# Decoder block on one core: pooling and gate arithmetic of VectorE dealt out in pieces, and nine low weight parts taken from the DMA to VectorE

## The chip, the core and the metric

The kernel runs on one core of a Trainium2 chip. A core has TensorE (PE) for matrix products, VectorE (DVE), ScalarE (ACT) and GpSimd (POOL) for element-wise work, SyncE (SP) which here only starts transfers, and 16 DMA engines. Each engine takes its instructions strictly in the order in which the program lists them, and waits on semaphores for what other engines or transfers have to finish first. The metric is the device time of one execution in microseconds, lower is better.

## What is computed

One block of a hybrid decoder on 528 positions (16 learned meta tokens and 512 real ones) of width 1024. Cut to what matters for the change, with its names:

```python
p = rmsnorm(h) @ w_in
q, k, v, glr, r, u, ga, gb = split(p)
o = gated_linear_attention(q, k, v, glr)            # chunks of 64, four heads
y_a = (rmsnorm(o) * silu(r)) @ w_a
# four groups of 256 channels, trailing mean over 2, 4, 8, 16 positions, minus the token
pooled = [mean_w(u[g]) - u[g] for g, w in enumerate((2, 4, 8, 16))]
y_b = (concat(pooled[g] @ w_pool_grp[g]) * pool_scale) @ w_b
h = h + (sigmoid(ga + b_a) * y_a + sigmoid(gb + b_b) * y_b) @ w_o
up = causal_conv3(rmsnorm(h) @ w_up)
h = h + (silu(up[:, :2816]) * up[:, 2816:]) @ w_down
out = rmsnorm(h)[16:]
```

All of it is float32. To get this accuracy from TensorE, an operand is split into a high part, which is its rounding to `fp32r`, and a low part, which is the operand minus the high part; a product is then three products: high by high, high weight by low data, low weight by high data.

## The kernel before, in words

Channels lie on the 128 partitions and positions on the free axis. The program has three stretches: projections for the attention (k, q, v, r) and the attention itself, then a list of units called `seq`, and at the end the last parts of the down product and the final norm. The change is in the units.

**Units.** A unit makes 256 output channels. Its number below is its place in `seq`: 0 is u0, 1 to 3 are a0 to a2, 4 is u1, 5 is u2, 6 is a3, 7 is u3, 8 to 11 are ga0 to ga3, 12 to 14 are gb0 to gb2, 15 is the grouped product grp, 16 is b0, 17 is gb3, 18 to 20 are b1 to b3, 21 to 24 are o0 to o3, and from 25 on come the 22 up units with the down units among them. A number after a name in the rows below (`gl10`, `sh_10a`, `x9`) is the number of the unit it belongs to; the profile itself leaves most of these numbers out.

**Plain and fast units.** A `plain` unit (L663) does eight products over two column halves. A `fast` unit (L695) is one level of a Strassen-like scheme: seven block products in place of eight, made by `seven`, into four PSUM banks `x`, `y`, `q` and `v`. Banks `x` and `q` are used more than once: the product into `x` that begins the unit (weights `gh` and `gl`) is read out by ScalarE (L710, "z11"), and only when it has been read does the second product into `x` (weights `sh_…a` and `sl_…a`) go on from the bank's contents. The same holds for L713 (z22), L716 (z12), L718 and L720 on VectorE, and L722 (z21) at the unit's end.

**Weights of a unit.** `fetch` loads a unit's raw weights (1 MB) into one of three buffers `raw`. `make_high` rounds three of its four blocks into `gh` on ScalarE (L607). `make_low` makes the low part `gl`: ScalarE writes the negated high part into it (L597), and three transfers started by GpSimd add the raw weights onto it from DRAM (L599, `accum_op=add`). `make_sums` makes the block sums: four additions in place on VectorE (L624), then high parts `sh_…a`, `sh_…b` on ScalarE and low parts `sl_…a`, `sl_…b` on VectorE (L269 and L270, the two lines of the helper `split`). `gh`, `gl` and the `s` tiles have two buffers each, so `sh_…b` of a unit cannot be written before the unit ahead of it is done with its own.

**When they are made.** In unit n, `fast` asks for the high part and the sums of unit n+1 behind z11, and `prepare` asks for the low part of unit n+2 behind z21. Between these edges the scheduler of the framework sets the order on each engine from the order of the code and its own estimate of times.

**Pooling and gates.** `pool_tree(g)` runs on VectorE behind a u unit: g+1 additions of shifted copies (L768), for g = 3 also two short operations (L766, L771), then the mean minus the token (L773), and `split` into `pah` on ScalarE and `pal` on VectorE. In the ga units VectorE also multiplies `ya` by the gate (L862), behind the sigmoids of ScalarE (L787).

**The start.** VectorE and GpSimd add up the squares for the first norm (L246 to L248); GpSimd also fills four constant tiles there (L299 to L301 and L309).

Of the kernel before, what the change touches and what calls it, by code (L numbers as in the profile page):

```python
# [1 line left out]

# [9 lines left out]
I32 = mybir.dt.int32  # L12
AF = mybir.ActivationFunctionType
ALU = mybir.AluOpType
# [4 lines left out]
T0 = 14  # L19
# [20 lines left out]
CROSS_X = {(0, 0): 0, (0, 1): 1, (1, 0): 2, (1, 1): 3}  # L40
# [30 lines left out]
def f32(ap):  # L71
    return ap.bitcast(F32)
# [3 lines left out]
def hybrid_block(ctx: ExitStack, tc: tile.TileContext, xt, g1d, wts, wsq, wdown, wglr, wgk, vecs, out):  # L76
    nc = tc.nc
    act, dve, pool, pe, sp = nc.scalar, nc.vector, nc.gpsimd, nc.tensor, nc.sync
# [153 lines left out]
    sq1 = big("sq1")  # L232
# [12 lines left out]
    for k in (2, 4, 6):  # L245
        pool.tensor_tensor(sq1[0], sq1[0], sq1[k], ALU.add)  # L246
        dve.tensor_tensor(sq1[1], sq1[1], sq1[k + 1], ALU.add)
    dve.tensor_tensor(sq1[0], sq1[0], sq1[1], ALU.add)  # L248

    def rsqrt_mean(dst, acc, cols, n, tmp):  # L250
        for src, c in parts_of(acc, cols):
# [16 lines left out]
    def split(hi, lo, src):  # L268
        act.activation(hi, src, AF.Copy)  # L269
        dve.tensor_tensor(lo, src, f32(hi), ALU.subtract)  # L270
# [25 lines left out]
    e1, e2 = flat("early1", lastp), flat("early2", lastp)  # L296
    reset, gk, kend0 = e1[:, 0:L], e1[:, 528:1040], e2[:, 0:512].rearrange("p (h c) -> p h c", h=4)
    glr_raw = e2[:, 512:640].rearrange("p (k c) -> p k c", k=KT)
    pool.memset(reset, 1.0)  # L299
    pool.memset(reset[:, 16 : 16 + 3 * 128 + 1 : 128], 0.0)  # L300
    pool.memset(gk, 0.0)  # L301
    for i in range(6):
        sp.dma_start(gk[16 * i : 16 * i + 16], wgk)
    sp.dma_start(vec, vecs)
# [1 line left out]
    glr_w = flat("glr_w", lastp, F32R, 1024).rearrange("p (k c) -> p k c", k=KT)  # L306
    gkg = flat("gkg", lastp, F32R)
    gk_r, glr = gkg[:, 0:512], gkg[:, 512:1040]
    pool.memset(glr_w.bitcast(I32), 0)  # L309
    stack = glr_w[:, :, 0:96].rearrange("p k (j i c) -> p k j i c", j=3, i=2)  # L310
    raw3 = glr_raw.unsqueeze(2).to_broadcast([P, KT, 3, 16])
    act.activation(stack[:, :, :, 0], raw3, AF.Copy)
# [5 lines left out]
    for k in range(KT):  # L318
        for m in range(2):
            hi, lo = preps[m]  # L320
# [95 lines left out]
    o = Whole("o")  # L416
# [129 lines left out]
    seq = [("plain", "u", 0)] + [("plain", "a", i) for i in range(3)]  # L546
# [11 lines left out]
    loaded, own, sums = {}, {}, {}  # L558
# [17 lines left out]
    low_made, high_made = set(), set()  # L576

    def direct_tiles(n):
# [9 lines left out]
                own[n] = [blocks(t) for t in hl], hl, None  # L588
        return own[n]

    def make_low(n):
        if n >= len(seq) or seq[n][0] == "down" or n in low_made:
            return
        low_made.add(n)
        _, (hi, lo), _ = direct_tiles(n)
        kind, name, i = seq[n]
        act.activation(lo, loaded[n][:, 0:3], AF.Copy, scale=-1.0)  # L597
        for b in (2, 0, 1) if kind == "fast" else (0, 1, 2) if name == "grp" else (1, 2, 0):
            pool.dma_start(lo[:, b], wsq[UNIT[name] + i, :, b], accum_op=ALU.add)  # L599

    def make_high(n):
        if n >= len(seq) or n in high_made:
            return
        high_made.add(n)
        _, (hi, lo), k = direct_tiles(n)
        if k is None:
            act.activation(hi, loaded[n][:, 0:3], AF.Copy)  # L607
        else:
            split(hi, lo, loaded[n].rearrange("p a b -> p (a b)")[:, 0:k])

# [3 lines left out]
    def make_sums(n):  # L614
        if n >= len(seq) or n in sums or seq[n][0] == "down":
            return
        raw = loaded[n]
        if seq[n][0] == "plain":
            x = two(f"{n}x")
            split(*(t[:, 0:1] for t in x), blocks(raw[:, 3:4]))  # L620
            sums[n] = (x,)
            return
        for dst, x in ((0, 3), (3, 2), (2, 0), (1, 2)):
            dve.tensor_tensor(raw[:, dst], raw[:, dst], raw[:, x], ALU.add)  # L624
        sums[n] = (two(f"{n}a"), two(f"{n}b"))
        split(*sums[n][0], blocks(raw[:, 0:3:2]))
        split(*sums[n][1], blocks(raw[:, 1:4:2]))
# [13 lines left out]
    def prepare(n, ins=None):  # L641
        fetch(n + 2)
        fetch(n + 3)
        behind(ins, make_low, n + 2)
# [24 lines left out]
    def plain(n, i, xh, xl, cols, evict, cross=None):  # L669
        w = weights(n)  # L670
        make_high(n + 1)
        make_sums(n + 1)
        for c in range(2):
            evict(2 * i + c, plain_half(n, i, c, xh, xl, cols, w))
            if cross and (i, c) in cross[0]:
                cross[1](cross[0][i, c])
        prepare(n)

    def lattice(name, b, n, x):
# [12 lines left out]
    def seven(acc, w, block, x, at, n, first=True):  # L692
        for k in range(4):
            for e, (a, b) in enumerate(((0, 0), (0, 1), (1, 0))):
                pe.matmul(  # L695
                    acc[:, 0:n], w[a][:, block, k], x[k][b][:, at],
                    start=first and k == 0 and e == 0, stop=k == 3 and e == 2,
                    skip_group_check=not first,
                )

    def fast(n, z, sides, cols):
        direct, crossed = sides
        g, sa, sb = weights(n)
        z11, z12 = (z[:, 0, a:b] for a, b in cols)
        z21, z22 = (z[:, 1, a:b] for a, b in cols)
        x, y, q, v_ = (bank(f"{c}{n}") for c in "xyqv")
        w = cols[0][1] - cols[0][0]
        n_ = slice(0, w)
        seven(x, g, 2, direct, 2, w)
        behind(act.activation(z11, x[:, n_], AF.Copy), make_high, n + 1)  # L710
        make_sums(n + 1)
        seven(q, sa, 0, crossed, 1, w)
        act.activation(z22, q[:, n_], AF.Copy)  # L713
        seven(v_, g, 0, crossed, 3, w)
        seven(x, sa, 1, crossed, 2, w, False)
        act.activation(z12, x[:, n_], AF.Copy)  # L716
        seven(y, g, 1, direct, 0, w)
        dve.tensor_tensor(z11, y[:, n_], z11, ALU.add)  # L718
        seven(q, sb, 0, direct, 1, w, False)
        dve.tensor_tensor(z12, q[:, n_], z12, ALU.add)  # L720
        seven(x, sb, 1, crossed, 0, w, False)
        turned = act.activation(z21, x[:, n_], AF.Copy, scale=-1.0)  # L722
        dve.tensor_tensor(z22, z21, z22, ALU.subtract)
        dve.tensor_tensor(z21, v_[:, n_], z21, ALU.add)
        prepare(n, turned)
# [5 lines left out]
    pah, pal = big("pah", F32R, lastp), big("pal", F32R, unitp)  # L731
# [18 lines left out]
        sides_x[1].append(x)  # L750

    def pool_tree(g):
        cur = u.pair(g)
        need = T0
        starts = []
        for i in reversed(range(g + 1)):
            starts.append(need)
            need = max(0, need - (1 << i))
        starts = starts[::-1]
        temps = big(f"pt{g}", F32, lastp if g < 3 else unitp)  # L760
        for i in range(g + 1):
            d = 1 << i
            nxt = temps.pair(i % 2)
            a = starts[i]
            if a < d:
                dve.tensor_copy(nxt[:, :, a:d], cur[:, :, a:d])  # L766
                a = d
            dve.tensor_tensor(nxt[:, :, a:], cur[:, :, a:], cur[:, :, a - d : L - d], ALU.add)  # L768
            cur = nxt
        if g == 3:  # L770
            dve.tensor_scalar(cur[:, :, T0 : T0 + 1], cur[:, :, T0 : T0 + 1], 16.0 / (T0 + 1), None, ALU.mult)  # L771
        ug = u.pair(g)[:, :, T0:]
        dve.scalar_tensor_tensor(ug, cur[:, :, T0:], 1.0 / (2 << g), ug, ALU.mult, ALU.subtract)  # L773
        split(pah.pair(g)[:, :, T0:], pal.pair(g)[:, :, T0:], ug)

    def take_u(m, accs):
        scaled(u[m], accs, HALF)
# [62 lines left out]
    for n in range(len(seq)):  # L840
        kind, name, i = seq[n]
        if name == "up":
            break
        if name == "u" and kind == "plain":
            for k in range(4):
                load_x(k)
            plain(n, i, xh, xl, HALF, take_u)
            ya = Whole("ya")
        elif name == "a":
            plain(n, i, zh, zl, TAIL, take_a, (CROSS_X, cross_x))  # L850
            if i == 2:
                pool_tree(0)
            if i == 3:
                pool_tree(2)
        elif name == "u":
            fast(n, u.pair(i), sides_x, FULL)
            if i != 2:
                pool_tree(i)
        elif name == "ga":
            z, _ = unit_gate(n, i, name)  # L860
            y = ya.pair(i)[:, :, T0:]
            dve.tensor_tensor(y, y, z[:, :, T0:], ALU.mult)  # L862
        elif name == "gb":
            gbs[i] = unit_gate(n, i, name)
            if i == 3:
                table(LOG_EXP, gbs[i][1])
        elif name == "grp":
            unit_grp(n)
        elif name == "b":
            plain(n, i, pbh, pbl, TAIL, take_b)  # L870
            if i == 3:
                h2, h2h, h2l = big("h2", F32, unitp), big("h2h", F32R, lastp), big("h2l", F32R, lastp)
                for k in range(4):
                    pool.memset(h2.pair(k)[:, :, H0:T0], 0.0)
                    sp.dma_start(h2.pair(k)[:, :, T0:], xt[2 * k : 2 * k + 2, :, T0:].rearrange("k p t -> p k t"))
        elif name == "o":
            plain(n, i, mh, ml, TAIL, take_o)
# [214 lines left out]
```

## Time and profile before

| what | value |
|---|---|
| time, median of 3 runs (lowest, highest) | 847.96 us (847.6, 849.24) |
| the profiled execution's own time | 848.24 us |
| its span, first to last instruction | 846.2 us |
| mean granted TensorE clock | 0.99 |
| low-part transfers by GpSimd (L599) | 141, 256 KB each |
| ScalarE copies into `gl` (L597) | 47 |

The profile is one execution. Times in it are microseconds from the span's start, unless marked ns. A row of the timeline gives start, duration, engine, line, operation, output and inputs, and in brackets how long the engine had stood idle before it and what ended that idle time. A row of groups gives the same work summed over all its instructions: busy time, mean ns of one, idle time before. The view of waits sums, for each pair of lines, how long the one waited for the other: total, number of times, longest. The view by stretches gives for each stretch the busy time of PE, its weight loads, VectorE, ScalarE and GpSimd, then the granted TensorE clock and the share of the DMA engines in use. The line numbers are those of the kernel before.

### The profile page before, as it was taken

What the parts mean: (1) busy time and instruction counts of PE and PEld (TensorE: products, weight loads), DVE (VectorE), ACT (ScalarE), POOL (GpSimd) and SP (SyncE); (2) the same over time, 40 slices, a digit from 0 to 9 for tenths busy, and PEclk for the clock granted to TensorE, in tenths of its full rate; (3) what the DMA queues carried; (4) which work ended last, traced back from release to release, by engine and by line L of the source; (5) the groups of instructions that cost most, each with busy time, mean ns of one, the idle gap of its engine ahead of it and who ended that gap; (6) DMA issues with size and microseconds to landing.
All of it is one profiled execution on the core that took longest, in us unless ns stands there. A gap on an engine that the chain in (4) does not pass through costs nothing.

```text
span 846.2 us, 15000 instructions
## 1 busy us (share of the span) xinstructions
PE 817.5 (97%) x6219; PEld 786.4 (93%) x6219; DVE 581.3 (69%) x878; ACT 490.4 (58%) x688; POOL 152.7 (18%) x180
## 2 busy tenths in 40 slices
PE   8999999999989799999999999999999999999994
PEld 6999999999989799999999999999889989999883
DVE  6677346679756777664334498999659975899845
ACT  7287244585645476776334556776547844686542
POOL 4000000021221222222124422220122110320021
PEclk9999999999999999999999999999999999999997
DMA  6423220168665758886788656876547745675102
GB/s 214 156 64 101 86 75 27 51 178 232 162 161 120 175 119 180 170 210 171 161 218 208 149 139 130 187 154 185 142 130 149 156 125 163 153 169 140 50 25 100
DMA packets 39459, 120.23 MB, mean 142 GB/s; under 512 B 4352, under 2 KB 7168, under 8 KB 33376
## 3 DMA queue, kind: packets, MB, share of 16 engines
q1 hardware_dynamic: 17856, 81.26, 29.5%
q0 software_dynamic: 20304, 36.97, 26.6%
q8 instruction: 48, 0.79, 0.4%
q10 hardware_dynamic: 1232, 1.05, 0.4%
q14 instruction: 19, 0.16, 0.1%
HBM read 117.17 MB, written 2.10 MB: 141 GB/s over the span
## 4 chain that ended last, share of the span: by engine, by line
PE 82%; DMA 5%; DVE 5%; ACT 5%; issue 1%; POOL 0%; SPq 0%; DVEq 0%; ACTq 0%
PE pp L663 22%; PE pd L946 12%; PE x L695 11%; PE q L695 8%; PE pv L170 6%; PE pr L170 5%; DMA gl<-in_wsq_dram 5%; PE y L695 4%; PE v L695 4%; PE pq L170 3%; PE pe L946 2%; PE pk L170 1%; ACT gl L597 1%; PE po L468 1%; DVE pt L768 1%
## 5 line engine op out<-in xcount | busy, mean ns | idle before, releaser
L599 POOL DMA_DIRECT2D gl<-in_wsq_dram x141 | 127.4, 1214 | 561.1 <-ACT gl L597 489.1
L607 ACT ACTIVATE gh<-raw 128x1536 fp32r<-128x1536 f32 x47 | 69.8, 1485 | 63.9 <-PE pd L946 24.8
L624 DVE TENSOR_TENSOR raw<-raw 128x512 f32<-128x512 f32 x116 | 79.8, 688 | 30.0 <-ACT gh L607 17.6
L946 PE MATMUL pd<-g,gh 128*128 128x512 f32 (+1 forms) x304 | 93.4, 389 | 0.0
L597 ACT ACTIVATE gl<-raw 128x1536 fp32r<-128x1536 f32 x47 | 69.4, 1477 | 13.5 <-PE pp L663 8.0
L946 PEld LDWEIGHTS pd<-g,gh 128*128 128x128 f32 x304 | 56.4, 188 | 12.3
L946 PE MATMUL pd<-g,gl 128*128 128x512 f32 (+1 forms) x152 | 58.9, 388 | 0.0
L153 ACT ACTIVATE whi<-wraw 128x1024 fp32r<-128x1024 f32 (+2 forms) x28 | 25.9, 933 | 52.5 <-PE pv L170 25.8
L154 DVE TENSOR_TENSOR wlo<-wraw,whi 128x1024 fp32r<-128x1024 f32 (+2 forms) x28 | 30.5, 1099 | 6.4 <-ACT whi L153 5.2
L946 PEld LDWEIGHTS pd<-g,gl 128*128 128x128 f32 x152 | 28.5, 188 | 6.4
L931 ACT ACTIVATE cv<-z,vec 128x512 f32<-128x512 f32 x44 | 33.9, 811 | 0.0
L971 DVE TENSOR_TENSOR h<-pd,h 128x512 f32<-128x512 f32 x24 | 16.5, 689 | 24.9 <-PE pd L946 24.9
L932 DVE SCALAR_TENSOR_TENSOR cv<-z,vec,cv 128x512 f32<-128x512 f32 x44 | 32.2, 744 | 0.0
L933 DVE SCALAR_TENSOR_TENSOR cv<-z,vec,cv 128x512 f32<-128x512 f32 x44 | 32.1, 743 | 0.0
L270 DVE TENSOR_TENSOR gl<-raw,gh 128x1536 fp32r<-128x1536 f32 (+1 forms) x16 | 25.9, 1621 | 6.4 <-ACT gh L269 6.4
L269 ACT ACTIVATE gh<-raw 128x1536 fp32r<-128x1536 f32 (+1 forms) x16 | 22.0, 1376 | 12.0 <-PE pd L946 9.3
L170 PE MATMUL pv<-xh,whi 128*128 128x264 f32 x128 | 26.3, 287 | 0.0
L170 PE MATMUL pr<-xh,whi 128*128 128x258 f32 (+1 forms) x128 | 25.9, 284 | 0.0
L170 PE MATMUL pv<-xl,whi 128*128 128x264 f32 x128 | 25.9, 283 | 0.0
L170 PE MATMUL pv<-xh,wlo 128*128 128x264 f32 x128 | 25.9, 283 | 0.0
L170 PE MATMUL pr<-xh,wlo 128*128 128x258 f32 (+1 forms) x128 | 25.8, 283 | 0.0
L170 PE MATMUL pr<-xl,whi 128*128 128x258 f32 (+1 forms) x128 | 25.6, 281 | 0.0
(1279 smaller groups left out, 2943.1 us busy)
## 6 DMA issues: line engine op xcount, KB each, us to landing
raw<-in_wsq_dram SPq DMA_DIRECT2D x47, 1024.0 KB, 5.9
gl<-in_wsq_dram POOLq DMA_DIRECT2D x141, 256.0 KB, 7.5
wraw<-in_wts_dram SPq DMA_DIRECT2D x22, 512.0 KB, 3.6
raw<-in_wdown_dram SPq DMA_DIRECT2D x12, 768.0 KB, 4.3
xb<-in_xt_dram SPq DMA_DIRECT2D x4, 528.0 KB, 6.6
h<-in_xt_dram SPq DMA_DIRECT2D x4, 514.0 KB, 11.4
raw<-in_wdown_dram SPq DMA_DIRECT2D x4, 512.0 KB, 3.5
x<-in_xt_dram SPq DMA_DIRECT2D x7, 264.0 KB, 6.5
```

What stands on the lines that cost most here:

```text
L154: dve.tensor_tensor(lo[:, a:b], t[:, a:b], f32(hi[:, a:b]), ALU.subtract)
L170: pe.matmul(acc[:, s, : b - a], w, x[:, a:b], start=(i == 0 and w is wh and x is xh), stop=(i == n - 1 and last),)
L597: act.activation(lo, loaded[n][:, 0:3], AF.Copy, scale=-1.0)
L599: pool.dma_start(lo[:, b], wsq[UNIT[name] + i, :, b], accum_op=ALU.add)
L607: act.activation(hi, loaded[n][:, 0:3], AF.Copy)
L624: dve.tensor_tensor(raw[:, dst], raw[:, dst], raw[:, x], ALU.add)
L663: pe.matmul(acc[:, 0 : b - a], w[p], q[k][:, a:b], start=k == 0 and e == 0, stop=k == KT - 1 and e == 2,)
L695: pe.matmul(acc[:, 0:n], w[a][:, block, k], x[k][b][:, at], start=first and k == 0 and e == 0, stop=k == 3 and e == 2, skip_group_check=no ...
L931: act.activation(cv, z[:, c, META:], AF.Identity, scale=v1("cw2", m), bias=v1("cb", m))
L932: dve.scalar_tensor_tensor(cv, z[:, c, META - 1 : L - 1], v1("cw1", m), cv, ALU.mult, ALU.add)
L933: dve.scalar_tensor_tensor(cv, z[:, c, META - 2 : L - 2], v1("cw0", m), cv, ALU.mult, ALU.add)
L946: pe.matmul(acc, w[p][:, c, k], gated[k0 + k][q][:, a:b], start=k == 0 and e == 0, stop=k == nk - 1 and e == 2,)
```

## The change

Four things are changed.

1. `pool_tree` no longer issues its VectorE work at once. It puts each addition, and the mean minus the token, as a piece into a queue `extras`, and no longer splits into `pah` and `pal`: `pool_split` does that, as a piece of its own, for group 0 behind u0, for groups 1 and 2 behind u2, and for group 3 behind u3.
2. `spare` takes pieces from the queue: one at two places in each fast unit, two in each half of the a units, and whatever is left ahead of grp. The gate product of `ya` (L862 before) goes to the front of the same queue.
3. For grp, b0 to b3 and o0 to o3 (nine units) `make_low` does nothing; `make_high` makes `gl` on VectorE as the raw weights minus `gh`. Nine ScalarE copies and 27 transfers go, nine VectorE subtractions of 128x1536 come.
4. The four fills at the start are put inside `tc.issue_after(summed.ins)`, which sets an edge behind the last addition of the squares, an instruction on VectorE; the fills are on GpSimd.

```diff
-    dve.tensor_tensor(sq1[0], sq1[0], sq1[1], ALU.add)
+    summed = dve.tensor_tensor(sq1[0], sq1[0], sq1[1], ALU.add)
...
-    pool.memset(reset, 1.0)
-    pool.memset(reset[:, 16 : 16 + 3 * 128 + 1 : 128], 0.0)
-    pool.memset(gk, 0.0)
+    with tc.issue_after(summed.ins):
+        pool.memset(reset, 1.0)
+        pool.memset(reset[:, 16 : 16 + 3 * 128 + 1 : 128], 0.0)
+        pool.memset(gk, 0.0)
...
-    pool.memset(glr_w.bitcast(I32), 0)
+    with tc.issue_after(summed.ins):
+        pool.memset(glr_w.bitcast(I32), 0)
...
+    def split_here(n):
+        return seq[n][0] == "down" or seq[n][1] in ("grp", "b", "o")
+
     def make_low(n):
-        if n >= len(seq) or seq[n][0] == "down" or n in low_made:
+        if n >= len(seq) or split_here(n) or n in low_made:
             return
...
         if k is None:
             act.activation(hi, loaded[n][:, 0:3], AF.Copy)
+            if split_here(n):
+                dve.tensor_tensor(lo, loaded[n][:, 0:3], f32(hi), ALU.subtract)
...
             if cross and (i, c) in cross[0]:
                 cross[1](cross[0][i, c])
+            elif cross is None or cross[0] is CROSS_X:
+                spare(2)
...
+    extras = deque()
+
+    def spare(k=1):
+        for _ in range(min(k, len(extras))):
+            extras.popleft()()
...
         behind(act.activation(z11, x[:, n_], AF.Copy), make_high, n + 1)
         make_sums(n + 1)
+        spare()
         seven(q, sa, 0, crossed, 1, w)
...
         dve.tensor_tensor(z12, q[:, n_], z12, ALU.add)
+        spare()
         seven(x, sb, 1, crossed, 0, w, False)
...
-        for i in range(g + 1):
+
+        def add(i):
             d = 1 << i
+            cur = temps.pair((i - 1) % 2) if i else u.pair(g)
             nxt = temps.pair(i % 2)
...
-        ug = u.pair(g)[:, :, T0:]
-        dve.scalar_tensor_tensor(ug, cur[:, :, T0:], 1.0 / (2 << g), ug, ALU.mult, ALU.subtract)
-        split(pah.pair(g)[:, :, T0:], pal.pair(g)[:, :, T0:], ug)
+
+        def less():
+            cur = temps.pair(g % 2)
...
+        extras.extend([partial(add, i) for i in range(g + 1)] + [less])
+
+    def pool_split(g):
+        extras.append(partial(split, *(t.pair(g)[:, :, T0:] for t in (pah, pal, u))))
+
+    def gate_a(i, z):
+        y = ya.pair(i)[:, :, T0:]
+        dve.tensor_tensor(y, y, z[:, :, T0:], ALU.mult)
...
             ya = Whole("ya")
+            pool_tree(0)
+            pool_split(0)
         elif name == "a":
             plain(n, i, zh, zl, TAIL, take_a, (CROSS_X, cross_x))
-            if i == 2:
-                pool_tree(0)
-            if i == 3:
-                pool_tree(2)
         elif name == "u":
             fast(n, u.pair(i), sides_x, FULL)
-            if i != 2:
-                pool_tree(i)
+            pool_tree(i)
+            for g in {2: (1, 2), 3: (3,)}.get(i, ()):
+                pool_split(g)
         elif name == "ga":
             z, _ = unit_gate(n, i, name)
-            y = ya.pair(i)[:, :, T0:]
-            dve.tensor_tensor(y, y, z[:, :, T0:], ALU.mult)
+            extras.appendleft(partial(gate_a, i, z))
...
         elif name == "grp":
+            spare(len(extras))
             unit_grp(n)
```

What this does to the order of instructions shows at three places. The line numbers in the rows of the change are those of the changed file: its L604, L614, L727, L734, L741 and L817 are L597, L607, L710, L716, L722 and L787 of the kernel before, and its L271 is L269.

ScalarE, from the end of unit 4 (u1) into unit 5 (u2), before; `u2_2906<-x5_2907` with L710 is z11 of unit 5, and `pah1` is the high part of pooling group 1:

```order
L722 ACTIVATE u1_2784<-x4_2785 128x264
L597 ACTIVATE gl6_2892<-raw6_2764 128x1536
L269 ACTIVATE pah1_2902<-u1_2779 128x2x514
L710 ACTIVATE u2_2906<-x5_2907 128x264
L607 ACTIVATE gh6_2891<-raw6_2764 128x1536
L713 ACTIVATE u2_2906<-q5_2909 128x264
```

The same place of the change:

```order
L741 ACTIVATE u1_2779<-x4_2780 128x264
L604 ACTIVATE gl6_2892<-raw6_2771 128x1536
L727 ACTIVATE u2_2897<-x5_2898 128x264
L614 ACTIVATE gh6_2891<-raw6_2771 128x1536
L731 ACTIVATE u2_2897<-q5_2900 128x264
L271 ACTIVATE sh_6x_2916<-raw6_2771 128x512
L734 ACTIVATE u2_2897<-x5_2898 128x264
L614 ACTIVATE gh7_3005<-raw7_2889 128x1536
L741 ACTIVATE u2_2897<-x5_2898 128x264
L604 ACTIVATE gl7_3006<-raw7_2889 128x1536
L271 ACTIVATE pah1_3011<-u1_2779 128x2x514
```

`pah1` has moved from ahead of z11 of unit 5 to behind the whole of that unit. The high part of group 3 moves likewise, from ahead of z11 of unit 8 into unit 10.

ScalarE, in unit 9 (ga1) and over its end into unit 10 (ga2), before; L722 on `x9` is z21, the last read of unit 9, `sh_10a` and `sh_10b` are block sums of unit 10, and L710 on `x10` is z11 of unit 10:

```order
L716 ACTIVATE ga1_3403<-x9_3404 128x264
L269 ACTIVATE sh_10a_3426<-raw10_3261 128x1024
L787 ACTIVATE ga1_3403<-ga1_3403,vec_102 128x514
L269 ACTIVATE sh_10b_3428<-raw10_3261 128x1024
L722 ACTIVATE ga1_3403<-x9_3404 128x264
L597 ACTIVATE gl11_3516<-raw11_3392 128x1536
L710 ACTIVATE ga2_3524<-x10_3525 128x264
```

The same place of the change:

```order
L734 ACTIVATE ga1_3394<-x9_3395 128x264
L741 ACTIVATE ga1_3394<-x9_3395 128x264
L604 ACTIVATE gl11_3510<-raw11_3384 128x1536
L271 ACTIVATE sh_10a_3417<-raw10_3259 128x1024
L271 ACTIVATE sh_10b_3419<-raw10_3259 128x1024
L817 ACTIVATE ga1_3394<-ga1_3394,vec_102 128x514 x2
L727 ACTIVATE ga2_3517<-x10_3518 128x264
```

`sh_10a` stood ahead of unit 9's last read and now stands behind it and behind the copy into `gl11`; `sh_10b` and both sigmoids stand between `sh_10a` and z11 of unit 10.

GpSimd at the start, in the change (`sq10` is the running sum of squares, `early1` holds two of the filled constants, `glr_w` another):

```order
L248 TENSOR_TENSOR sq10_155<-sq10_155,sq11_168 128x528
L302 MEMSET early1_206 128x528
L248 TENSOR_TENSOR sq10_155<-sq10_155,sq12_177 128x528
L303 MEMSET early1_206 128x4
L304 MEMSET early1_206 128x512
L387 MEMSET early2_207 128x512
L248 TENSOR_TENSOR sq10_155<-sq10_155,sq13_182 128x528
L313 MEMSET glr_w_219 128x1024
```

These eight rows stand in the same order, with the same neighbours, in the kernel before: nothing has moved on GpSimd here.

More of the change, by code (lines that the diff above doesn't have):

```diff
@@ L1 @@
+from collections import deque
 from contextlib import ExitStack
+from functools import partial
 import concourse.bass as bass
@@ L752, in pool_tree @@
     def pool_tree(g):
-        cur = u.pair(g)
         need = T0
@@ L768, in pool_tree @@
             dve.tensor_tensor(nxt[:, :, a:], cur[:, :, a:], cur[:, :, a - d : L - d], ALU.add)
-            cur = nxt
-        if g == 3:
-            dve.tensor_scalar(cur[:, :, T0 : T0 + 1], cur[:, :, T0 : T0 + 1], 16.0 / (T0 + 1), None, ALU.mult)
-        ug = u.pair(g)[:, :, T0:]
-        dve.scalar_tensor_tensor(ug, cur[:, :, T0:], 1.0 / (2 << g), ug, ALU.mult, ALU.subtract)
-        split(pah.pair(g)[:, :, T0:], pal.pair(g)[:, :, T0:], ug)
+        def less():
+            cur = temps.pair(g % 2)
+            if g == 3:
+                dve.tensor_scalar(cur[:, :, T0 : T0 + 1], cur[:, :, T0 : T0 + 1], 16.0 / (T0 + 1), None, ALU.mult)
+            ug = u.pair(g)[:, :, T0:]
+            dve.scalar_tensor_tensor(ug, cur[:, :, T0:], 1.0 / (2 << g), ug, ALU.mult, ALU.subtract)
+        extras.extend([partial(add, i) for i in range(g + 1)] + [less])
[4 more added lines that the diff above has]
+        dve.tensor_tensor(y, y, z[:, :, T0:], ALU.mult)
     def take_u(m, accs):
```

## The prediction

> **What bounds the kernel now.** I read the page's busy times first, then the waits of TensorE.
>
> ```profile
> span 846.2 us, 15000 instructions
> PE 817.5 (97%) x6219; PEld 786.4 (93%) x6219; DVE 581.3 (69%) x878; ACT 490.4 (58%) x688; POOL 152.7 (18%) x180
> PE x L695 <- ACT ga L710: 5.3, 1, 5.3
> PE x L695 <- ACT u L710: 3.9, 1, 3.9
> PE x L695 <- DMA gl<-in_wsq_dram: 1.6, 2, 1.2
> PE pp L663 <- DMA gl<-in_wsq_dram: 0.5, 1, 0.5
> ```
>
> TensorE is busy for 97% of the span and the change takes no product away, so only its idle time, 846.2 - 817.5 = 28.7 us, and its clock can give anything. Two single waits make 9.2 us of it, both for ScalarE's read z11 (L710). The timeline of the two places, TensorE and ScalarE:
>
> ```profile
> 247.01 1.48 ACT L597 ACTIVATE gl<-raw 128x1536 fp32r<-128x1536 f32 x1
> 252.73 1.06 ACT L269 ACTIVATE pah<-u 128x1028 fp32r<-128x1028 f32 x1 [4.24 <-DVE u L773]
> 255.15 0.39 ACT L710 ACTIVATE u<-x 128x264 f32<-128x264 f32 x1 [1.35 <-DVE pal L270]
> 255.59 0.39 PE L695 MATMUL x<-xxh,sh_5a 128*128 128x264 f32 x1 [3.94 <-ACT u L710]
> ...
> 284.62 1.48 ACT L597 ACTIVATE gl<-raw 128x1536 fp32r<-128x1536 f32 x1
> 293.21 1.06 ACT L269 ACTIVATE pah<-u 128x1028 fp32r<-128x1028 f32 x1 [7.11 <-DVE u L773]
> 294.17 0.37 ACT L710 ACTIVATE ga<-x 128x264 f32<-128x264 f32 x1
> 294.60 0.59 PE L695 MATMUL x<-xxh,sh_8a 128*128 128x264 f32 x1 [5.34 <-ACT ga L710]
> ```
>
> ScalarE had finished its copy at 248.5 and stood for 4.24 us with `pah` at the head of its queue, because `pah` needs the end of VectorE's pooling tree (L773); z11 of unit 5 stood behind it. Behind the second tree, one addition longer per group, it is 7.11 us. The first time z11 also had to wait for `pal`. The two waits cost more than themselves, as the stretches show (busy PE comes first, the clock stands after the five engines):
>
> ```profile
> 256.00:258.00 2.00, 2.00 (x13) 2.00 (x13) 0.00 (x1) 2.00 (x3) 0.00 (x0) 0.65 0.96 175
> 258.00:260.00 2.00, 2.00 (x11) 2.00 (x11) 0.69 (x1) 1.36 (x3) 0.00 (x0) 0.50 0.01 1
> 294.00:296.00 2.00, 1.40 (x6) 1.41 (x7) 1.62 (x3) 2.00 (x4) 0.00 (x0) 0.53 0.69 124
> 296.00:298.00 2.00, 2.00 (x13) 2.00 (x12) 1.93 (x3) 0.56 (x2) 0.00 (x0) 0.61 0.00 0
> 546.00:548.00 2.00, 1.50 (x12) 1.50 (x13) 2.00 (x4) 2.00 (x4) 0.00 (x0) 1.00 0.40 71
> ```
>
> After the first wait the clock lost 2.00 x 0.35 + 2.00 x 0.50 = 1.7 us, after the second 1.40 x 0.47 + 2.00 x 0.39 = 1.4 us. After a wait of 1.2 us (the longest of the first transfer row, at 546) it lost nothing.
>
> **Pooling dealt out (removed waits).** In the order of the change neither `pah1` nor `pah3` stands ahead of the next z11, and its z11 of unit 5 waits for TensorE alone. z11 of unit 5 then follows the copy at 248.5 and is done by 248.9. What is late next? Groups of twelve products follow each other so:
>
> ```profile
> 326.38 1.46 PE x L695 x12
> 327.84 1.48 PE y L695 x12
> 329.32 1.48 PE q L695 x12
> ```
>
> so the second product into `x`, now the fourth group, comes three groups, 4.4 us, after the unit's start, near 250.0 for unit 5 and, counted likewise, 1.3 us after z11 for unit 8. Both waits go whole: 3.94 + 1.7 + 5.34 + 1.4 = 12.4 us.
>
> The work itself stays, on VectorE:
>
> ```profile
> L768 DVE TENSOR_TENSOR pt<-pt 128x1028 f32<-128x1028 f32 x3 | 3.7, 1225 | 0.1
> L862 DVE TENSOR_TENSOR ya<-ya,ga 128x1028 f32<-128x1028 f32 x4 | 4.9, 1230 | 2.3 <-ACT ga L787 2.3
> 302.00:376.00 74.00, 73.38 (x598) 72.62 (x597) 47.87 (x78) 56.81 (x82) 18.55 (x21) 1.00 0.84 189
> ```
>
> The group 3 tree moves three additions, the mean and the split (5 x 1.23 = 6.2 us on VectorE, one copy on ScalarE) into units 8 to 13. That stretch has VectorE busy for 47.87 of 74 us, so there is room on average; a queue can still be late at one place, which is the next term.
>
> **A new wait in unit 10.** In the order rows of the change, `sh_10a` comes behind z21 of unit 9 and the copy into `gl11`. z21 needs unit 9's last product. Prices from start to start:
>
> ```profile
> 312.58 0.37 ACT L722 ACTIVATE ga<-x 128x264 f32<-128x264 f32 x1
> 312.85 1.48 ACT L597 ACTIVATE gl<-raw 128x1536 fp32r<-128x1536 f32 x1
> 314.23 0.37 ACT L710 ACTIVATE ga<-x 128x264 f32<-128x264 f32 x1
> 310.05 1.06 ACT L269 ACTIVATE sh_10a<-raw 128x1024 fp32r<-128x1024 f32 x1 [1.70 <-DVE raw L624]
> ```
>
> From the unit's start about 0.1 (semaphore), z21 0.27, the copy 1.38, `sh_10a` 1.06: ready at 2.8 to 2.9. TensorE asks for it after its first group, at 1.46. It waits 1.4 us. Behind `sh_10a` in that queue stand `sh_10b`, two sigmoids and z11 of unit 10, which ends near 5.4; TensorE, late by 1.4, wants it at 5.9, so it adds nothing. By unit 11 ScalarE is back: its queue there has about 0.5 us to spare. The wait is shorter than 3.94 and hardly longer than 1.2 us, so its clock cost lies between 0 and 1.7; I take 0, the row that it is nearest to.
>
> The Trainium skill, "TensorE: Matmul & The Clock Gate" (What's actually happening), says that the clock falls to half after an idle window of about 3.4 us. The trace agrees as far as it goes (half after 3.94, full after 1.2); by that rule the 1.4 us cost no clock, which is the same 0.
>
> **Low parts by VectorE.** Nine copies (L597, 1.48 us each, 13.3 us) leave ScalarE, 27 transfers leave GpSimd and the DMA, nine subtractions come to VectorE:
>
> ```profile
> L270 DVE TENSOR_TENSOR gl<-raw,gh 128x1536 fp32r<-128x1536 f32 x12 | 21.0, 1753 | 5.7 <-ACT gh L269 5.7
> 376.00:476.00 100.00, 99.72 (x833) 99.52 (x834) 43.78 (x65) 46.10 (x53) 31.90 (x37) 1.00 0.75 180
> ```
>
> 9 x 1.75 = 15.8 us, where VectorE is busy for 43.78 of 100 us; a weight made one unit ahead has most of a unit's 10 to 11 us to spare. The 0.5 us wait at 376.28 was for `gl16` (b0), now made by VectorE in unit 14: it goes, 0.5 us. One subtraction lies in a path: that of `gl22` stands between b3's eviction and the addition of `ya`, from which `mh3` and `ml3` for o0 are made.
>
> ```profile
> 432.07 1.23 DVE L822 TENSOR_TENSOR gb<-gb,ya 128x1028 f32<-128x1028 f32 x1
> 433.78 1.05 ACT L269 ACTIVATE mh<-gb 128x1028 fp32r<-128x1028 f32 x1
> 434.86 1.23 DVE L270 TENSOR_TENSOR ml<-gb,mh 128x1028 fp32r<-128x1028 f32 x1 [0.26 <-ACT mh L269]
> ```
>
> L822 then starts at 433.8 and ends at 435.0, `mh` ends at 436.0, `ml` at 437.3. The scheduler answered by pulling later products of o0 ahead: the first use of `mh3` is its 41st product, that of `ml3` its 51st, at 0.12 us each near 435.9 and 437.1. I charge 0.3 us; bounds 0 and 1.7, the whole subtraction.
>
> **Transfers.** In unit 11 TensorE waited 0.4 us (the other half of the 1.6) for `gl11`:
>
> ```profile
> 314.62 7.26 DMA gl<-in_wsq_dram
> 366.46 9.78 DMA gl<-in_wsq_dram
> ```
>
> With unit 10 late by 1.4 us and `gl11` copied earlier in it, that wait goes: 0.4 us. `gl10` now comes 0.6 us too late at 7.26, but that lies inside unit 10's wait. The 1.2 us at 546 is in the up units, which the change leaves alone; it stays.
>
> **The fills.** The order of GpSimd at the start has not moved, so 0 us. Its edge names an instruction of another engine. So for this part the change does not do what it says, and neither gains nor costs anything.
>
> **The sum.** -12.4 - 0.5 - 0.4 + 1.4 + 0.3 = -11.6 us. The profiled execution took 848.24 us (span 846.2 and 2.04 around it), 0.28 above the median of the runs. 848.24 - 11.6 = **836.6 us**.
>
> **Rivals.**
>
> - *Unit 10 does not wait.* If `sh_10a` is ready in time, 836.6 - 1.4 = 835.2. For it: the estimate hangs on one place in the order. Against it: the order is fixed, and z21 cannot come before unit 9's end. 0.12.
> - *ScalarE stays late.* Its queue in gate units carries 8 to 9 us in units of 10.3; if unit 10's lateness is not made up in unit 11, each of units 11 to 14 pays 1.4 again: 836.6 + 5.6 = 842.2. For it: sigmoids now stand ahead of z11 in units 12 and 13, with no slack by my count. Against it: 56.81 busy of 74 us, and the spare 0.5 us in unit 11. 0.14.
> - *The gain is eaten by VectorE.* The pieces stand ahead of the block sums (L624) that ScalarE needs for `sh`; if each of units 8 to 14 is late by one piece and a half, 7 x 1.7 = 11.9, about 848.5. Against it: the room above. 0.04.
> - *Slower: the accumulating transfers become the bound.* Without the two stops the units follow closely, and a `gl` must land within 6.7 us of its issue for unit 10, about 7.4 for units 12 to 14, 7.8 for unit 6, 9.2 for units 7 and 8. If all land as late as the second row of transfers (9.78 and 0.54 of issue, 10.3 us) the lateness is 3.6 + 3 x 2.9 + 2.5 + 2 x 1.1 = 17.0, less the 1.4 already counted: 836.6 + 15.6 = 852.2. It decides from a landing time of about 10.0 us on. Against it: the page's median landing is 7.5 us over 141 transfers. 0.03.
>
> The Trainium skill, "DMA: Bandwidth & Descriptors" (Anatomy of one DMA), gives 2.0 us plus bytes over 436 GB/s, by my estimate 2.6 us for 256 KB, with which no such wait could occur and the last rival would have no chance. The trace's 7.26 speaks against it for these transfers, so it keeps its 0.03.
>
> **How the numbers follow.** The forecast has 0.62, the rivals 0.12, 0.14, 0.04 and 0.03; 0.05 is left for losses of 2 to 4 us that I have not seen. The range goes from 834.2 (unit 10 does not wait, and a further 1 us goes) to 842.6 (ScalarE late to the end, or a full clock loss and the whole subtraction on top of the forecast: 836.6 + 1.7 + 1.4 = 839.7). A measurement of this kernel can tell 0.2%, 1.7 us, from no change. Faster: 0.62 + 0.12 + 0.14 + 0.05 = 0.93; within 0.2%: 0.04; slower: 0.03.
>
> **What would show it.** In the profile of the change: no wait of TensorE for L710's successor above 0.5 us, and a clock of 1.00 between 240 and 300; a wait of about 1.4 us of a `q` product for `sh_10a`; none for `gl16`; idle time of TensorE near 28.7 - 9.28 - 0.5 - 0.4 + 1.4 + 0.3 = 20.2 us. A wait above 3 us anywhere in units 5 to 14, or a clock below 1.00 there, would make the forecast wrong.

## The result, and the profile after

| kernel | median (lowest to highest, runs) | ratio, 95% interval |
|---|---|---|
| before | 848.52 us (847.6 to 849.24, 4) | |
| the change | 834.27 us (832.76 to 836.4, 4) | 0.9835, 0.981 to 0.986 |

The profiled execution of the change took 836.4 us, the slowest of its four, with a span of 834.7 us; that of before had 848.24 and 846.2. The first lines of its page:

```profile
span 834.7 us, 14943 instructions
PE 813.1 (97%) x6219; PEld 783.2 (94%) x6219; DVE 593.8 (71%) x887; ACT 477.9 (57%) x679; POOL 128.9 (15%) x153
```

TensorE's busy time fell by 4.4 us with the same 6219 products, its idle time by 7.1 us, from 28.7 to 834.7 - 813.1 = 21.6 us. What TensorE waited for in the change (total, times, longest):

```profile
PE x L706 <- DMA gl<-in_wsq_dram: 1.6, 3, 1.2
...
PE pp L672 <- DMA gl<-in_wsq_dram: 1.2, 3, 0.5
...
PE q L706 <- ACT sh_10a L271: 0.9, 1, 0.9
```

Neither z11 (L727 now) nor `gl16` is in that view; `sh_10a` is new, and so are more waits for `gl` transfers. Units 5 and 8 in the timeline of the change:

```profile
247.34 1.48 ACT L604 ACTIVATE gl<-raw 128x1536 fp32r<-128x1536 f32 x1
248.72 0.38 ACT L727 ACTIVATE u<-x 128x264 f32<-128x264 f32 x1
250.35 0.28 PE L706 MATMUL x<-xxh,sh_5a 128*128 128x264 f32 x1
...
279.96 1.48 ACT L604 ACTIVATE gl<-raw 128x1536 fp32r<-128x1536 f32 x1
281.34 0.38 ACT L727 ACTIVATE ga<-x 128x264 f32<-128x264 f32 x1
282.97 0.28 PE L706 MATMUL x<-xxh,sh_8a 128*128 128x264 f32 x1
```

In both units z11 follows the copy without a gap and ends 1.25 us before TensorE comes back to the bank. The stretches over these units (the granted clock, the share of its full clock that TensorE is given, is the number behind the five engines):

```profile
246.00:262.00 16.00, 15.55 (x129) 15.35 (x128) 12.16 (x16) 9.77 (x12) 5.29 (x6) 1.00 0.81 202
...
280.00:300.00 20.00, 19.79 (x161) 19.55 (x160) 17.34 (x26) 12.97 (x19) 5.29 (x6) 1.00 0.78 170
```

The clock stays at 1.00, as it does over all of 240 to 300. Unit 10, where the prediction put the new wait:

```profile
299.40 0.39 ACT L741 ACTIVATE ga<-x 128x264 f32<-128x264 f32 x1 [3.38 <-PE x L706]
299.69 1.48 ACT L604 ACTIVATE gl<-raw 128x1536 fp32r<-128x1536 f32 x1
299.81 0.39 PE L706 MATMUL x<-dhx,gl 128*128 128x264 f32 x1 [0.21 <-DMA gl<-in_wsq_dram]
301.07 1.04 ACT L271 ACTIVATE sh_10a<-raw 128x1024 fp32r<-128x1024 f32 x1
302.16 0.39 PE L706 MATMUL q<-xxh,sh_10a 128*128 128x264 f32 x1 [0.86 <-ACT sh_10a L271]
```

z21, the copy into `gl11` and `sh_10a` stand one behind the other. TensorE's first group was held by the late `gl10`, so that only 0.86 us of the wait is for `sh_10a`.

Where the time went shows best unit by unit. The table gives the start of the first product with a block sum of that unit's weights, from the timelines of the two kernels:

| unit | before | change | difference | since the row above |
|---|---|---|---|---|
| 0 (u0) | 195.92 | 195.68 | -0.24 | |
| 4 (u1) | 236.83 | 237.16 | +0.33 | +0.57 |
| 6 (a3) | 268.00 | 263.34 | -4.66 | -4.99 |
| 8 (ga0) | 284.69 | 280.04 | -4.65 | +0.01 |
| 9 (ga1) | 301.83 | 290.42 | -11.41 | -6.76 |
| 10 (ga2) | 312.35 | 302.16 | -10.19 | +1.22 |
| 11 (ga3) | 323.26 | 312.48 | -10.78 | -0.59 |
| 15 (grp) | 371.63 | 360.74 | -10.89 | -0.11 |
| 16 (b0) | 381.64 | 370.05 | -11.59 | -0.70 |
| 22 (o1) | 449.32 | 437.87 | -11.45 | +0.14 |
| span | 846.2 | 834.7 | -11.5 | -0.05 |

### The profile page after: what moved, and what is told of

It is laid out like the page before. It is cut to its first block, busy times and chain, and to the rows that moved or that the text cites. A ratio compares the mean times of both kernels' runs of the same rounds, so it can differ in the third digit from the quotient of the medians.

```text
span 834.7 us, 14943 instructions
## 1 busy us (share of the span) xinstructions
PE 813.1 (97%) x6219; PEld 783.2 (94%) x6219; DVE 593.8 (71%) x887; ACT 477.9 (57%) x679; POOL 128.9 (15%) x153
## 4 chain that ended last, share of the span: by engine, by line
PE 85%; DMA 6%; DVE 3%; ACT 3%; issue 1%; POOL 1%; SPq 0%; DVEq 0%; ACTq 0%
PE pp L672 18%; PE x L706 14%; PE pd L975 12%; PE q L706 9%; PE pv L172 6%; DMA gl<-in_wsq_dram 5%; PE y L706 5%; PE v L706 5%; PE pr L172 4%; PE pq L172 3%; PE pe L975 2%; PE pk L172 2%; PE pgrp L834 1%; PE po L472 1%; ACT gl L604 1%
## 5 line engine op out<-in xcount | busy, mean ns | idle before, releaser
L606 POOL DMA_DIRECT2D gl<-in_wsq_dram x114 | 102.0, 1207 | 500.3 <-ACT gl L604 421.9
L614 ACT ACTIVATE gh<-raw 128x1536 fp32r<-128x1536 f32 x47 | 69.9, 1486 | 61.0 <-PE pp L672 26.7
L604 ACT ACTIVATE gl<-raw 128x1536 fp32r<-128x1536 f32 x38 | 56.2, 1478 | 9.3 <-issue 4.4
L271 ACT ACTIVATE gh<-raw 128x1536 fp32r<-128x1536 f32 (+1 forms) x16 | 22.0, 1377 | 11.8 <-PE pd L975 9.1
```

## The experiments

Ratios are to the kernel before, run on the same chip in turn; its median was 848 to 849 us each time. The experiments ran on three chips, so their ratios compare better than their times. In the rows of these kernels a line number can stand a few lines off.

### Which part of the change carries it

The change without its low parts by VectorE:

```diff
     def split_here(n):
-        return seq[n][0] == "down" or seq[n][1] in ("grp", "b", "o")
+        return seq[n][0] == "down"
```

> The change without its third part: the low parts of grp, b and o are made by ScalarE's copy and GpSimd's transfers again. Theory (two waits and the clock behind them carry the gain): both stops of units 5 and 8 stay away, unit 10 still waits 0.9 to 1.4 us for sh_10a, and the wait for gl16 comes back with 0.5 to 0.7 us: 0.7 us above the change, about 835 us beside 834.3. Rival (the transfers and copies that are gone carry a good part, by freeing DMA engines and ScalarE): 841 us or more.

Measured: 834.38 us (834.02 to 840.02, 5 runs), ratio 0.9842 (0.9818 to 0.9865). The gain is all there. Its profile has 0.39 us of wait for `gl16` again and 0.59 us for `sh_10a`.

The low parts alone, put into the kernel before:

```diff
-        if n >= len(seq) or seq[n][0] == "down" or n in low_made:
+        if n >= len(seq) or split_here(n) or n in low_made:
...
             act.activation(hi, loaded[n][:, 0:3], AF.Copy)
+            if split_here(n):
+                dve.tensor_tensor(lo, loaded[n][:, 0:3], f32(hi), ALU.subtract)
```

> The kernel before with the third part alone: nine low parts by VectorE, pooling and gates as before. Theory: the waits of 3.9 and 5.3 us and the clock dips behind them stay; the wait for gl16 goes: 0.5 to 0.7 us below the kernel before, about 847.8 us beside 848.5. Rival (the freed DMA and ScalarE carry a good part): 843 us or less.

Measured: 847.78 us (11 runs), ratio 0.9984 (0.997 to 0.9998), as the theory has it. The waits of 3.94 and 5.34 us stand in its profile unchanged. The clock behind the second one does not:

```profile
292.00:294.00 2.00, 0.26 (x1) 0.26 (x2) 0.87 (x2) 1.65 (x3) 0.00 (x0) 0.50 1.11 201
294.00:296.00 2.00, 2.00 (x10) 2.00 (x11) 1.89 (x4) 1.34 (x2) 0.00 (x0) 0.50 0.21 37
296.00:298.00 2.00, 2.00 (x11) 2.00 (x10) 1.89 (x3) 1.06 (x2) 0.00 (x0) 0.50 0.00 0
298.00:300.00 2.00, 2.00 (x15) 2.00 (x14) 1.57 (x2) 0.39 (x1) 0.00 (x0) 0.79 0.00 0
```

The loss here is 0.26 x 0.50 + 2.00 x 0.50 + 2.00 x 0.50 + 2.00 x 0.21 = 2.55 us, where the same stop of 5.34 us cost 1.4 us in the profile of the kernel before.

The change with the additions in one block again:

```diff
-        extras.extend([partial(add, i) for i in range(g + 1)] + [less])
+        for i in range(g + 1):
+            add(i)
+        less()
```

> The change with the pooling additions issued at once, as one block behind each u unit, and only the split into pah and pal and the gate products left in the queue. Theory (the place of pah in ScalarE's queue made the waits): no stop at z11 of units 5 and 8; the block of group 3 (5 instructions of 1.15 us) stands ahead of unit 9's block sums instead, so sh_9a comes behind z21 of unit 8 and TensorE waits about 3.0 us for it and some 1.7 us for z11 of unit 9; unit 10's wait of 0.9 to 1.4 us goes. About 3.3 us above the change, 837.6 us (up to 839.5 with a clock dip). Rival (the additions have to be dealt out for the waits to go): stops of 3.9 and 5.3 us as before, 846 us or more.

Measured: 834.94 us (834.54 to 837.88, 4 runs), ratio 0.9839 (0.9824 to 0.9855): not slower than the change by anything that this measurement can tell. The theory held, its price did not:

```profile
290.34 1.05 ACT L271 ACTIVATE sh_9a<-raw 128x1024 fp32r<-128x1024 f32 x1
...
290.46 0.68 DVE L633 TENSOR_TENSOR raw<-raw 128x512 f32<-128x512 f32 x1
...
291.44 0.39 PE L706 MATMUL q<-xxh,sh_9a 128*128 128x264 f32 x1 [0.81 <-ACT sh_9a L271]
```

`sh_9a` needs three of the four block sums, and the fourth (290.46) ends after it has started; I had let it wait for all four. So the wait is 0.81 us, not 3.0, and z11 of unit 9 came in time.

The kernel before with nothing but the two splits moved:

```diff
-        split(pah.pair(g)[:, :, T0:], pal.pair(g)[:, :, T0:], ug)
+        held.append((pah.pair(g)[:, :, T0:], pal.pair(g)[:, :, T0:], ug))
+        if g in (0, 2):
+            split_held()
+
+    held = []
+
+    def split_held():
+        while held:
+            split(*held.pop(0))
...
             if i != 2:
                 pool_tree(i)
+            else:
+                split_held()
...
             dve.tensor_tensor(y, y, z[:, :, T0:], ALU.mult)
+            if i == 1:
+                split_held()
```

> The kernel before with one edit: the splits into pah and pal of groups 1 and 3 come later (group 1 behind unit 5, group 3 in unit 9); the additions stay in a block, gates, low parts and fills as before. Theory (these two places are the whole gain): no stop at z11 of units 5 and 8, the clock stays at 1.00 there, waits for sh_9a (about 0.8 us, as with the tree in a block) and gl16 (0.5 us) remain: 836 us, from 834.5 to 838. Rival (dealing out the additions, the gate products or the low parts by VectorE carry part of it): 841 us or more.

Measured: 835.79 us (834.59 to 836.95, 4 runs), ratio 0.9847 (0.9828 to 0.9865). Two wait rows of its profile, and the clock over units 5 and 8:

```profile
291.58 0.39 PE L695 MATMUL q<-xxh,sh_9a 128*128 128x264 f32 x1 [1.17 <-ACT sh_9a L269]
...
354.29 0.51 PE L812 MATMUL pgrp<-pah,gl 128*128 128x258 f32 x2 [0.86 <-DMA gl<-in_wsq_dram]
```

```profile
246.00:262.00 16.00, 15.96 (x131) 15.75 (x130) 11.96 (x16) 9.77 (x12) 5.29 (x6) 1.00 0.82 205
...
280.00:300.00 20.00, 18.83 (x152) 18.41 (x151) 18.11 (x27) 13.78 (x18) 5.30 (x6) 1.00 0.76 172
```

Two moved instructions on ScalarE, and with them their partners on VectorE, give the change's time within what can be told apart. The fills need no run: without `issue_after` there each engine's instructions and their waits are the same, one for one.

### Does a stop of TensorE cost clock by its length?

A stop of chosen length, by more copies of the same PSUM block ahead of z11 of unit 5 in the change (9, 14, 17 or 20 of them):

```diff
         seven(x, g, 2, direct, 2, w)
+        if n == 5:
+            for _ in range(9):
+                act.activation(z11, x[:, n_], AF.Copy)
```

> The change with nine more copies of the same PSUM block by ScalarE, 0.27 us each, ahead of z11 of unit 5, so that TensorE stops there for about 2.5 us. Theory (only a stop near 4 us takes the clock down): 2.5 us lost and a granted clock of 1.00 behind it. Rival (any stop costs clock in proportion, or the dip came from what else runs there): a clock near 0.7 for some 3 us behind it, 1 us more.

> The same with fourteen more copies, so that TensorE stops for about 3.9 us, as in the kernel before, but for another reason. Theory (the length of the stop takes the clock down): 3.9 us lost and a clock of 0.5 to 0.65 for some 4 us behind it, 1.7 us more. Rival (the dip of the kernel before belonged to the pooling or the transfers beside it): a clock of 1.00, nothing more than the 3.9 us.

These two missed their lengths: with more copies the scheduler put the group into `y`, and of the second group into `q` five products (9 copies) or all twelve (14 and more), ahead of the second one into `x`. That gave z11 about 2 and 3 us more time. The stops were 0.51 and 1.75 us, the clock 1.00 in both; the longer one:

```profile
254.13 0.39 PE L706 MATMUL x<-xxh,sh_5a 128*128 128x264 f32 x1 [1.75 <-ACT u L730]
```

```profile
256.00:258.00 2.00, 2.00 (x19) 2.00 (x19) 0.62 (x2) 1.63 (x3) 0.00 (x0) 1.00 0.38 67
```

> The change with seventeen more copies ahead of z11 of unit 5. Nine and fourteen copies made stops of 0.51 and 1.75 us; each further copy adds about 0.42 us, so this one is about 3.0 us. Theory (the length of the stop takes the clock down, somewhere between 1.75 and 3.94 us): either a clock of 1.00 or a dip behind it, which narrows the place. Rival (no length of stop does it in this kernel): a clock of 1.00 here and behind a stop of 4.3 us too.

> The same with twenty more copies, for a stop of about 4.3 us, a little longer than that of unit 5 in the kernel before (3.94 us). Theory (the length of the stop takes the clock down): a granted clock of 0.5 to 0.65 for some 4 us behind it, about 1.7 us lost on top of the stop. Rival (the dip of the kernel before belonged to the pooling or the transfers beside it): a clock of 1.00 and nothing lost but the stop.

With 17 copies:

```profile
255.56 0.39 PE L706 MATMUL x<-xxh,sh_5a 128*128 128x264 f32 x1 [3.03 <-ACT u L730]
```

```profile
256.00:258.00 2.00, 2.00 (x11) 2.00 (x10) 0.00 (x0) 2.00 (x2) 0.00 (x0) 0.50 0.55 97
258.00:260.00 2.00, 2.00 (x14) 2.00 (x13) 1.03 (x2) 1.05 (x3) 0.00 (x0) 0.66 0.00 0
260.00:262.00 2.00, 2.00 (x19) 2.00 (x18) 0.00 (x0) 0.00 (x0) 0.00 (x0) 1.00 0.73 188
```

With 20:

```profile
257.12 0.45 PE L706 MATMUL x<-xxh,sh_5a 128*128 128x264 f32 x1 [4.28 <-ACT u L730]
```

```profile
258.00:260.00 2.00, 2.00 (x11) 2.00 (x10) 0.00 (x0) 2.00 (x3) 0.00 (x0) 0.50 0.00 0
260.00:262.00 2.00, 2.00 (x15) 2.00 (x15) 1.03 (x2) 0.71 (x2) 0.00 (x0) 0.82 0.00 0
```

The stop of 1.75 us cost no clock, that of 3.03 us 2.00 x 0.50 + 2.00 x 0.34 = 1.7 us. That of 4.28 us cost 2.00 x 0.50 + 2.00 x 0.18 = 1.4 us in these two rows and 0.3 us more ahead of them, from 257.12 on, so 1.7 us as well. So a stop of this length brings the dip without any pooling work beside it. In stretches of half a microsecond the clock stands at 0.50 for 3.4 us in each of these two dips and in both of the kernel before, and at 1.00 on either side. Its fall comes 3.4 to 4.9 us after TensorE stopped, in three of the four only when TensorE was at work again, and in the kernel before with the low parts alone the dip behind the stop of 5.34 us is 6.8 us long. So the loss does not follow from the length of the stop alone. Each length was run once and at one place: where the limit lies between 1.75 and 3.03 us, and whether it is the same at every moment, stays open. The single times (835.62, 836.34, 839.52 and 839.51 us for 9, 14, 17 and 20 copies) come from two chips and vary too much to price a stop by: 20 copies came out no slower than 17.

### What is left between the units

One piece less in unit 9, which brings `sh_10a` ahead of z21:

```diff
         make_sums(n + 1)
-        spare()
+        if n != 9:
+            spare()
         seven(q, sa, 0, crossed, 1, w)
```

> The change with the first of the two pieces left out in unit 9 (each later piece moves on by one place), so that sh_10a stands ahead of z21 of unit 9 on ScalarE. Theory (unit 10's wait is the place of sh_10a): that wait goes and nothing takes its place, 1.4 to 1.5 us below the change, about 832.8 us. Rival (ScalarE is short of time in these units, and the wait only moves to a later z11 or sh): the time of the change, 834.3 us.

Measured: 836.09 us (834.51 to 840.84, 5 runs), ratio 0.9853 (0.983 to 0.9875), so no gain. The profile:

```profile
297.27 1.06 ACT L271 ACTIVATE sh_10a<-raw 128x1024 fp32r<-128x1024 f32 x1 [1.60 <-DVE raw L633]
299.05 0.39 ACT L743 ACTIVATE ga<-x 128x264 f32<-128x264 f32 x1 [0.72 <-PE x L706]
...
313.01 2.65 POOL L606 DMA_DIRECT2D gl<-in_wsq_dram  x3 [8.31 <-ACT gl L604]
...
321.31 0.39 PE L706 MATMUL x<-dhx,gl 128*128 128x264 f32 x1 [0.90 <-DMA gl<-in_wsq_dram]
```

`sh_10a` is ready early and its wait is gone, but two units later TensorE stands for `gl12`, whose transfers were issued from 313.01 on. By the first product with a block sum, this kernel is 1.13 us ahead of the change in unit 10 (301.03 against 302.16) and 0.10 us in unit 12 (322.63 against 322.73): the gain of unit 10 was given back. The rival that I had named, ScalarE, was not what took it.

So the transfers were tried themselves. The copy that they follow waited for z21, though the buffer is free after the last product that reads it, a group of `q` and one of `x` earlier:

```diff
-    def prepare(n, ins=None):
+    def prepare(n, ins=None, early=False):
         fetch(n + 2)
         fetch(n + 3)
-        behind(ins, make_low, n + 2)
+        if not early:
+            behind(ins, make_low, n + 2)
...
+        fetch(n + 2)
+        make_low(n + 2)
         seven(q, sb, 0, direct, 1, w, False)
...
-        prepare(n, turned)
+        prepare(n, turned, True)
```

> The change with one edit: in a fast unit n the copy into gl of unit n+2 is asked for behind the last product that reads unit n's gl (bank y) and no longer behind z21, so its three transfers start some 2.9 us earlier; sh_10a then also stands ahead of z21 of unit 9. Theory (what is left between the units is the lateness of accumulating transfers that land 7.3 to 9.7 us after their issue): TensorE's waits for gl in fast units go, and unit 10's for sh_10a with them: 2.5 to 4 us below the change, about 831 us. Rival (the transfers land when the queue lets them, whenever they are issued, or ScalarE has no room for the earlier copy): the time of the change, 834.3 us or more.

Measured: 831.0 us (829.91 to 831.71, 5 runs), ratio 0.9786 (0.9769 to 0.9803), faster than both the kernel before and the change: its interval ends below that of the change. In unit 5:

```profile
254.70 1.47 ACT L604 ACTIVATE gl<-raw 128x1536 fp32r<-128x1536 f32 x1
256.37 0.39 ACT L744 ACTIVATE u<-x 128x264 f32<-128x264 f32 x1 [0.20 <-PE x L707]
```

The copy now stands ahead of z21 (L744 here). Unit 7's transfers start at 256.46 where they started at 258.48 in the change, 2.0 us earlier and not the expected 2.9, with TensorE at the same point of unit 5 within 0.1 us. TensorE's waits for `gl` in this kernel, all of them:

```profile
PE pp L673 <- DMA gl<-in_wsq_dram: 0.2, 1, 0.2
```

They were 1.6 + 1.2 = 2.8 us in the profile of the change.

With the earlier copies, two parts were taken out again. The low parts of grp, b and o by ScalarE and transfers (the first diff of this section, on top of the last):

> The kernel with the earlier copies (831.0 us) without the third part of the change: low parts of grp, b and o by ScalarE's copy and GpSimd's transfers. Theory (that part is worth the wait for gl16 and little else): 0.2 to 0.8 us more, about 831.5 us. Rival (with the other waits gone the 27 transfers stand in the way): 833 us or more.

Measured: 831.27 us (829.67 to 832.45, 4 runs), ratio 0.9796 (0.9774 to 0.9818). No difference that can be told.

And the kernel before with the two moved splits and the earlier copies alone:

> The kernel before with two edits only: the later splits of groups 1 and 3 (835.8 us) and the earlier copies into gl in fast units. Theory (these two places of ScalarE's queue are all that matters; dealing out, gate products, VectorE's low parts and the fills are worth 1 to 2 us together, the waits for sh_9a and gl16): about 832.8 us. Rival (the dealt-out pieces are what gives ScalarE room for the earlier copy): 835 us or more.

Measured: 833.41 us (832.84 to 834.53, 5 runs), ratio 0.9827 (0.9807 to 0.9848). Its profile has 1.27 us of wait for `sh_9a`, which is not in that of the kernel of 831.27 us, where the additions and gate products are dealt out and the splits stand at other places. So dealing out may be worth 2 us once the transfers are early: each of the four runs with it is faster than each of the five without. But the two intervals overlap, and of the 3.1 us between the two profiled spans 1.1 us lie ahead of unit 0, where the two kernels are alike.

## Why the prediction was right, and where its sizes were off

**The two stops and the clock (-12.4).** Right in cause and size. From unit 8 to unit 9 the change gains 6.76 us, where 5.34 + 1.4 was counted; from unit 4 to unit 6 it gains 4.99, where 3.94 + 1.7 = 5.64 was counted. Of the 0.65 that is missing, 0.45 is a wait for a `gl` in unit 6; the rest is not accounted for. Moving the two splits alone gives 0.9847. That a stop of this length brings a dip of the clock is shown by the stops made on purpose; how much it costs differs, since the second one cost 1.4 us in the profile of the kernel before and 2.55 us in that of the same kernel with the low parts.

**Unit 10 (+1.4).** It came where it was placed and for that reason, and cost 1.22 us. Of this the 0.86 is `sh_10a`; the prediction had let the late `gl10` vanish inside that wait, but it came ahead of it and took part of it. What the step did not see is that the wait is nearly free: taken away alone, it gave way to a later `gl` in the profile, and the time did not fall. The rival in which ScalarE stays late did not happen, since no wait for ScalarE follows in units 11 to 14.

**Low parts (-0.5 for `gl16`, +0.3 for o0) and `gl11` (-0.4).** `gl16`: 0.70 us from unit 15 to unit 16. o0: 0.14 us over units 16 to 22, near the lower bound, which suggests that the products that the scheduler had pulled ahead cover the subtraction. `gl11`: 0.59 us. The low parts alone, in the kernel before, give 0.9984; that interval reaches from 0.2 to 2.5 us, too wide to size 0.5 us by.

**Transfers, the term that was too small.** The prediction gave the accumulating transfers a chance of 0.03, priced at all of them landing after 10.3 us. The issue to landing of single ones in the change:

```profile
DMA to landing us min/median/max: 4.1/7.3/11.2
```

The median was as expected, and the spread was no wider than before (4.2 to 11.4 us there); it is single late ones that count once the units follow closely. Two of the waits that the kernel before does not have, ahead of unit 4 and in unit 6:

```profile
213.96 0.50 PE L672 MATMUL pp<-zh,gl 128*128 128x258 f32 x2 [0.48 <-DMA gl<-in_wsq_dram]
...
258.02 0.50 PE L672 MATMUL pp<-zh,gl 128*128 128x258 f32 x2 [0.45 <-DMA gl<-in_wsq_dram]
```

All told TensorE waits 2.8 us for `gl` in this profile, against 2.1 in that of before; 1.19 us of both is the same wait in the up units. The earlier copies show what they are worth with `sh_10a`: 834.27 - 831.0 = 3.3 us by the medians.

**The sum.** It was 836.6 us. The profiled execution took 836.4, with a span 11.5 us below that of before, where 11.6 was counted. That they agree so closely is luck: TensorE's idle time was to fall to 20.2 us and fell to 21.6, and its busy time fell by 4.4 us where the two dips account for 3.1; the two misses cancel. The rest of the busy time is not accounted for. By the medians the change gains 848.52 - 834.27 = 14.25 us, 2.65 more than counted, and 834.27 lies just above the range's lower end of 834.2. Two things can make up that difference, and neither is shown: the profiled execution of the change was the slowest of its four, and a dip can cost more than it did in the one profile of before. The transfers are a likely source of the spread, since TensorE's waits for `gl` range from none to 2.9 us in the profiles of the changed kernels; but these profiles also differ by 1.5 us in when unit 0 begins, and only one execution of each is profiled.

**The fills.** Nothing moved on GpSimd, as the order said.

**The rule on the clock.** The prediction held the figure of about 3.4 us for an idle window from the Trainium skill, "TensorE: Matmul & The Clock Gate" (What's actually happening), against the 1.4 us wait, and both gave no loss. The runs agree for the stop of 1.75 us and differ for that of 3.03 us, as the trace counts idle time, behind which the clock was already halved; the measurement decides.

## What to carry to other kernels

An instruction that waits for a long chain on another engine must not stand in a queue ahead of a short one that the busiest engine waits for; here moving two such instructions, with their partners, gave the gain of the whole change within what can be told apart. Cutting the chain into pieces added nothing that could be measured; it may be worth 2 us once the transfers are early as well. Where waits for different producers lie close together along a tight sequence, removing one may only uncover the next: read how late the second one would be before pricing the first. Start an accumulating transfer at the last read of its buffer, not at the end of the unit: here that gave 3.3 us, the wait for `sh_10a` included.

## What the runs showed of the hardware

TensorE's granted clock fell to 0.50 after a stop of 3.03 us and stayed at 1.00 after one of 1.75 us. The dips behind the stops of 3.03, 3.94, 4.28 and 5.34 us lasted 3.4 us each and cost 1.7, 1.7, 1.7 and 1.4 us; in the kernel before with the low parts alone the one behind a stop of 5.34 us lasted 6.8 us and cost 2.55 us. Transfers of 256 KB that add onto what their target holds landed 4.1 to 11.2 us after their issue within one execution, a spread that is larger than most of the terms of this case.
